# A softmax kernel's two places where stores follow loads: a small head on the store replaced by a small tail on the load

## The chip, the cores and the metric

The kernel runs on one core of one Trainium2 chip. The metric is device time in microseconds (us). Before the change it is 163.16 us, the median of 3 runs (162.55 to 163.5).

## What is computed

The input `x` has shape 16 x 1024 x 512 in float32, that is 16,384 rows of 512. Each row is divided by a temperature of 0.5 and goes through a softmax:

```python
x_scaled = x / temp                                   # temp = 0.5
x_max = np.max(x_scaled, axis=-1, keepdims=True)
exp_x = np.exp(x_scaled - x_max)
return (exp_x / np.sum(exp_x, axis=-1, keepdims=True)).astype(np.float32)
```

33.55 MB are read from HBM and 33.55 MB are written to it.

## The kernel before

The rows are cut into 8 chunks (0 to 7) of 128 partitions x 16 rows x 512. A partition's 16 rows lie one after another in HBM, so a whole chunk is 4096 KB, and each partition's part of it is one run of 32 KiB. Six SBUF tiles hold chunks (`BUFS = 6`). Chunks 6 and 7 are loaded into the tiles of chunks 0 and 1, and must wait until those are stored.

The order of the work is written out by hand, engine by engine. For each block (chunk 0 is worked on in three blocks, chunk 7 in two, the others whole):

- `shift` (L74 to L82), VectorE (DVE): the negated maximum of every row (L78), then times 2 (L82).
- `exponentials` (L103 to L118), ScalarE (ACT): for each row, exp(2x - 2max) in place, with the sum of the row (L109).
- `scale_vector` (L121 to L132), DVE: the reciprocal of the sums (L126), then 14 of 16 rows are multiplied by it (L128). `scale_scalar` (L134 to L143), ACT: the other rows (L139).
- `store` (L145 to L154): the chunk goes to HBM once its last block is done (L152).

All loads (L71) and all stores (L152) are issued by SyncE (SP), in one queue, in this order: the loads of chunks 0 to 5 at the start; store 0; store 1; the load of chunk 6 (waits until store 0 has landed); the load of chunk 7 (waits until store 1 has landed); stores 2 to 7. SP issues in order, so an instruction of its that waits holds up all that stand behind it. A DMA takes its turn in the queue once it is issued. There are thus two places in the queue where a store comes directly after a load: load 5 then store 0, and load 7 then store 2. And one where a load comes after a store: store 1 then load 6.

`LOADS` says how each chunk's load is cut: chunk 0 in three (rows 0 to 3, 4 to 7, 8 to 15), chunks 1 to 6 whole, chunk 7 without its last row. That row is loaded by GpSimd (POOL) in `load_last_row` (L89 to L101), through another queue (q0), when ACT is at row 10 of chunk 5.

`STORES` says how each store is cut, in columns of a partition's 16 x 512 values. Stores 0 and 2 use `LEAD`: a first DMA of 128 columns (512 bytes of each partition, 64 KB in all, "the head"), then a second with the rest (32,256 bytes of each partition, 4032 KB). The others are one DMA each (32,768 bytes of each partition). A partition's part of a DMA is one packet in the trace, and 8 partitions go through each of the 16 DMA engines. Each DMA ends with a completion packet of 4 bytes on each engine; it has landed when all 16 have been written.

SP's DMAs count their completions in eight semaphores, taken in turn; the ninth DMA uses the first one's again, and waits until the first has landed.

Of the kernel before, what the change touches and what calls it, by code (L numbers as in the profile page):

```python
# [1 line left out]

# [4 lines left out]


@with_exitstack
def kernel(  # L10
    ctx: ExitStack,
    tc: tile.TileContext,
    x: bass.AP,
    out: bass.AP,
):
    nc = tc.nc
    fp32 = mybir.dt.float32
    P = nc.NUM_PARTITIONS
    AX = mybir.AxisListType.X
    EXP = mybir.ActivationFunctionType.Exp  # L20
    COPY = mybir.ActivationFunctionType.Copy
    MAX = mybir.AluOpType.max

    D = x.shape[-1]
    xf = x.flatten_outer_dims()
    of = out.flatten_outer_dims()
    N = xf.shape[0]

    G = 16
    C = N // (P * G)
    assert C * P * G == N
    xr = xf.rearrange("(c p g) d -> c p g d", p=P, g=G)
    outr = of.rearrange("(c p g) d -> c p g d", p=P, g=G)
    WHOLE = [(0, G)]
    LOADS = [[(0, 4), (4, 8), (8, G)]] + [WHOLE] * 6 + [[(0, G - 1)]]
    BLOCKS = [[(0, 4), (4, 8), (8, G)]] + [WHOLE] * 6 + [[(0, 8), (8, G)]]

    LEAD = [(0, D // 4), (D // 4, G * D)]
    ALL = [(0, G * D)]
    STORES = [LEAD, ALL, LEAD] + [ALL] * 5
    BMAX = 16
    BUFS = 6

    data = ctx.enter_context(tc.tile_pool(name="data", bufs=BUFS))
    stats = ctx.enter_context(tc.tile_pool(name="stats", bufs=6))

    ctx.enter_context(tc.manual_schedule())  # L50


    warm = stats.tile([P, 1], fp32, name="warm", bufs=1)
    zero = nc.const_aps.tensor(0.0, (P, 1), fp32)
    nc.scalar.activation(out=warm, in_=zero, func=EXP)  # L55

    chunks = {}
    blocks = [(c, lo, hi) for c in range(C) for lo, hi in BLOCKS[c]]
    n = len(blocks)
    biases, sums, recips = {}, {}, {}  # L60

    finished = []

    def load(c):
        if c < BUFS:
            chunks[c] = data.tile([P, G, D], fp32, name="xt")
        else:
            chunks[c] = chunks[c - BUFS]
        xt = chunks[c]
        for lo, hi in LOADS[c]:  # L70
            part = nc.sync.dma_start(out=xt[:, lo:hi, :], in_=xr[c][:, lo:hi, :])  # L71
            finished.append(part.ins.name)

    def shift(i):  # L74
        c, lo, hi = blocks[i]
        b = hi - lo
        negmax = stats.tile([P, BMAX], fp32, name="negmax")
        nc.vector.tensor_reduce(  # L78
            negmax[:, 0:b], chunks[c][:, lo:hi, :], axis=AX, op=MAX, negate=True
        )  # L80
        biases[i] = stats.tile([P, BMAX], fp32, name="bias")
        nc.vector.tensor_scalar_mul(biases[i][:, 0:b], negmax[:, 0:b], 2.0)  # L82

    def load_last_row(signal):  # L89
        seen = stats.tile([P, 1], fp32, name="seen", bufs=1)  # L90
        copied = nc.gpsimd.tensor_copy(out=seen, in_=signal)  # L91
        finished.append(copied.ins.name)
        c = C - 1
        halves = "p (h d) -> p h d"
        to = chunks[c - BUFS][:, G - 1, :].rearrange(halves, h=2)
        of_ = xr[c][:, G - 1, :].rearrange(halves, h=2)
        for p0, p1 in ((P - 2, P), (0, P - 2)):
            part = nc.gpsimd.dma_start(  # L98
                out=to[p0:p1], in_=of_[p0:p1], max_dma_last_dim=2 * D
            )  # L100
            finished.append(part.ins.name)  # L101

    def exponentials(i, rows):  # L103
        c, lo, hi = blocks[i]
        if i not in sums:
            sums[i] = stats.tile([P, BMAX], fp32, name="sums")
        for g in rows:
            row = chunks[c][:, lo + g, :]
            nc.scalar.activation(  # L109
                out=row,  # L110
                in_=row,
                func=EXP,
                bias=biases[i][:, g : g + 1],
                scale=2.0,
                accum_out=sums[i][:, g : g + 1],
            )
            if c == BUFS - 1 and g == 10:
                load_last_row(sums[i][:, g : g + 1])  # L118


    def scale_vector(i):  # L121
        c, lo, hi = blocks[i]
        b = hi - lo
        k = b - b // 8
        recips[i] = stats.tile([P, BMAX], fp32, name="recip")
        nc.vector.reciprocal(recips[i][:, 0:b], sums[i][:, 0:b])  # L126
        rows = chunks[c][:, lo : lo + k, :]
        last = nc.vector.tensor_mul(  # L128
            rows, rows, recips[i][:, 0:k].unsqueeze(2).broadcast_to((P, k, D))
        )  # L130
        if i == n - 1:
            finished.append(last.ins.name)  # L132

    def scale_scalar(i):  # L134
        c, lo, hi = blocks[i]
        b = hi - lo
        for g in range(b - b // 8, b):
            row = chunks[c][:, lo + g, :]
            last = nc.scalar.activation(  # L139
                out=row, in_=row, func=COPY, scale=recips[i][:, g : g + 1]  # L140
            )
            if i == n - 1:
                finished.append(last.ins.name)  # L143

    def store(i):  # L145
        c, _, end = blocks[i]
        if end < G:
            return
        to = outr[c].rearrange("p g d -> p (g d)")
        of_ = chunks[c].rearrange("p g d -> p (g d)")  # L150
        for lo, hi in STORES[c]:
            part = nc.sync.dma_start(out=to[:, lo:hi], in_=of_[:, lo:hi])  # L152
            if c < C - 1:
                finished.append(part.ins.name)  # L154

    for c in range(BUFS):
        load(c)

    def rows(i):
        c, lo, hi = blocks[i]
        return range(hi - lo)

    shift(0)
    shift(1)
    exponentials(0, rows(0))
    for i in range(n):
        if i + 1 < n:
            exponentials(i + 1, rows(i + 1))  # L170
        scale_vector(i)
        scale_scalar(i)
        if i + 2 < n:
            shift(i + 2)
        store(i)
        c, _, hi = blocks[i]
        if hi == G and c == 1:
            load(BUFS)
            load(BUFS + 1)

    seen = nc.sync.nop()
    info = mybir.DependencyInfo(
        mybir.DependencyClass.Sync, mybir.DependencyReason.DATA
    )
    for name in finished:
        tc.add_manual_dep(seen.ins, name, info, reason="leaves one wait for the end")


# [1 line left out]
_INS = ['x']  # L190
_OUTS = [((16, 1024, 512), 'float32')]


# [23 lines left out]
```

## Time and profile before

| what | us |
|---|---|
| median of 3 runs | 163.16 (162.55 to 163.5) |
| the profiled execution's own time | 162.63 |
| its span, first to last instruction | 160.9 |
| DVE busy | 134.7 (84%) |
| ACT busy | 101.9 (63%) |
| DMA queue q1 (SP's): share of 16 engines' span | 97.4% |
| moved over the span | 67.13 MB, 417 GB/s |

The DMA queue is fullest: its packets fill 97.4% of the time of the 16 DMA engines. The SP timeline shows when each DMA was issued; the list of DMA issues shows how long after that the last of its 16 completions came, and their sum is the landing time. Where the queue always holds work, the interval from one landing to the next is the time that the slowest engine spent on that DMA. The packet records of the trace give the start, duration and size of each packet; they do not say which engine carried it.

### The profile page before, as it was taken

What the parts mean: (1) busy time and instruction counts of PE and PEld (TensorE: products, weight loads), DVE (VectorE), ACT (ScalarE), POOL (GpSimd) and SP (SyncE); (2) the same over time, 40 slices, a digit from 0 to 9 for tenths busy, and PEclk for the clock granted to TensorE, in tenths of its full rate; (3) what the DMA queues carried; (4) which work ended last, traced back from release to release, by engine and by line L of the source; (5) the groups of instructions that cost most, each with busy time, mean ns of one, the idle gap of its engine ahead of it and who ended that gap; (6) DMA issues with size and microseconds to landing.
All of it is one profiled execution on the core that took longest, in us unless ns stands there. A gap on an engine that the chain in (4) does not pass through costs nothing.

```text
span 160.9 us, 418 instructions
## 1 busy us (share of the span) xinstructions
DVE 134.7 (84%) x44; ACT 101.9 (63%) x273; POOL 1.9 (1%) x7
## 2 busy tenths in 40 slices
DVE  0589949999999999999999999999999999772000
ACT  3095490099899927993699459963999942950000
POOL 0000000000000000000000000300000000000000
DMA  5999999999999999999999999999999999999993
GB/s 183 444 428 493 407 407 489 407 391 491 407 407 464 432 399 393 393 428 473 399 424 473 394 466 411 410 466 439 416 416 432 456 416 432 456 416 416 464 416 139
DMA packets 3010, 67.13 MB, mean 417 GB/s; under 512 B 376, under 2 KB 632, under 8 KB 704
## 3 DMA queue, kind: packets, MB, share of 16 engines
q1 hardware_dynamic: 2880, 66.85, 97.4%
q0 software_dynamic: 128, 0.26, 0.4%
q14 instruction: 2, 0.02, 0.0%
HBM read 33.55 MB, written 33.55 MB: 417 GB/s over the span
## 4 chain that ended last, share of the span: by engine, by line
DVE 68%; DMA 13%; issue 5%; ACT 3%; SPq 1%
DVE negmax L78 38%; DVE xt L128 29%; DMA xt<-in_x_dram 13%; ACT xt L109 3%; DVE recip L126 1%; DVE bias L82 1%; SPq L71 1%
## 5 line engine op out<-in xcount | busy, mean ns | idle before, releaser
L109 ACT ACTIVATE xt<-xt,bias 128x512 f32<-128x512 f32 x128 | 90.4, 708 | 40.1 <-DVE bias L82 40.1
L78 DVE TENSOR_REDUCE negmax<-xt 128x16 f32<-128x8192 f32 (+2 forms) x11 | 69.9, 6352 | 7.9 <-DMA xt<-in_x_dram 7.9
L128 DVE TENSOR_TENSOR xt<-xt,recip 128x7168 f32<-128x7168 f32 (+2 forms) x11 | 62.0, 5636 | 0.4
L109 ACT ACTIVATION_READ_ACCUMULATOR xt<-xt,bias 128x1 f32 x128 | 24.0, 187 | 0.0
L139 ACT ACTIVATE xt<-xt,recip 128x512 f32<-128x512 f32 x15 | 9.9, 707 | 0.0
L126 DVE RECIPROCAL recip<-sums 128x16 f32<-128x16 f32 (+2 forms) x11 | 2.4, 219 | 2.3 <-ACT xt L109 2.3
L82 DVE TENSOR_SCALAR bias<-negmax 128x16 f32<-128x16 f32 (+2 forms) x11 | 1.9, 173 | 0.4
L55 ACT ACT_TABLE_LOAD x1 | 1.3, 1283 | 0.7 <-PEq L201 0.7
L98 POOL DMA_DIRECT2D xt<-in_x_dram x2 | 1.5, 741 | 0.6 <-issue 0.6
L91 POOL COPY seen<-sums 128x1 f32<-128x1 f32 x1 | 0.2, 184 | 102.0 <-ACT xt L109 102.0
L55 ACT ACTIVATE warm<-const-float32-0.0 128x1 f32<-128x1 f32 x1 | 0.2, 203 | 0.0
L201 POOL MEMSET const-bfloat16-1.0<- 128x1 bf16 x1 | 0.1, 96 | 0.0
L201 POOL MEMSET const-uint8-127<- 128x1 uint8 x1 | 0.1, 96 | 0.0
L201 POOL MEMSET const-float32-0.0<- 128x1 f32 x1 | 0.1, 93 | 0.2 <-issue 0.2
L201 POOL MEMSET const-float32-1.0<- 128x1 f32 x1 | 0.1, 93 | 0.0
## 6 DMA issues: line engine op xcount, KB each, us to landing
xt<-in_x_dram SPq DMA_DIRECT2D x6, 4096.0 KB, 34.4
out_dram<-xt SPq DMA_DIRECT2D x6, 4096.0 KB, 21.5
out_dram<-xt SPq DMA_DIRECT2D x2, 4032.0 KB, 28.6
xt<-in_x_dram SPq DMA_DIRECT2D x1, 3840.0 KB, 19.5
xt<-in_x_dram SPq DMA_DIRECT2D x2, 1024.0 KB, 6.1
xt<-in_x_dram SPq DMA_DIRECT2D x1, 2048.0 KB, 11.5
xt<-in_x_dram POOLq DMA_DIRECT2D x1, 252.0 KB, 13.7
out_dram<-xt SPq DMA_DIRECT2D x2, 64.0 KB, 34.2
```

The lines of the kernel that those rows point to most:

```text
L55: nc.scalar.activation(out=warm, in_=zero, func=EXP)
L71: part = nc.sync.dma_start(out=xt[:, lo:hi, :], in_=xr[c][:, lo:hi, :])
L78: nc.vector.tensor_reduce(negmax[:, 0:b], chunks[c][:, lo:hi, :], axis=AX, op=MAX, negate=True)
L82: nc.vector.tensor_scalar_mul(biases[i][:, 0:b], negmax[:, 0:b], 2.0)
L91: copied = nc.gpsimd.tensor_copy(out=seen, in_=signal)
L98: part = nc.gpsimd.dma_start(out=to[p0:p1], in_=of_[p0:p1], max_dma_last_dim=2 * D)
L109: nc.scalar.activation(out=row, in_=row, func=EXP, bias=biases[i][:, g : g + 1], scale=2.0, accum_out=sums[i][:, g : g + 1],)
L126: nc.vector.reciprocal(recips[i][:, 0:b], sums[i][:, 0:b])
L128: last = nc.vector.tensor_mul(rows, rows, recips[i][:, 0:k].unsqueeze(2).broadcast_to((P, k, D)))
L139: last = nc.scalar.activation(out=row, in_=row, func=COPY, scale=recips[i][:, g : g + 1])
L201: nc = _bacc.Bacc("TRN2", target_bir_lowering=False, num_devices=1)
```

## The change

Load 5 is cut in two DMAs: rows 0 to 14 (30,720 bytes of each partition), then row 15 (2,048 bytes of each partition, 256 KB in all, "the tail"). Load 7, which had rows 0 to 14 in one DMA, is cut into rows 0 to 13 (28,672 bytes) and row 14 (2,048 bytes). Stores 0 and 2 become one DMA each of 32,768 bytes of each partition. The number of DMAs on SP's queue stays 20. The rest of the program is the same but for which semaphores are waited for.

```diff
     WHOLE = [(0, G)]
-    LOADS = [[(0, 4), (4, 8), (8, G)]] + [WHOLE] * 6 + [[(0, G - 1)]]
+
+    LOADS = [[(0, 4), (4, 8), (8, G)]] + [WHOLE] * 4
+    LOADS += [[(0, G - 1), (G - 1, G)], WHOLE, [(0, G - 2), (G - 2, G - 1)]]
     BLOCKS = [[(0, 4), (4, 8), (8, G)]] + [WHOLE] * 6 + [[(0, 8), (8, G)]]
-
-    LEAD = [(0, D // 4), (D // 4, G * D)]
     ALL = [(0, G * D)]
-    STORES = [LEAD, ALL, LEAD] + [ALL] * 5
+    STORES = [ALL] * 8
```

SP's queue around the two places, with bytes of each partition:

| place | before | after |
|---|---|---|
| load 5, store 0 | 32,768; 512; 32,256 | 30,720; 2,048; 32,768 |
| load 7, store 2 | 30,720; 512; 32,256 | 28,672; 2,048; 32,768 |

## The prediction

> **What bounds the kernel now.** First the page's busy slices and its DMA queues.
>
> ```profile
> DVE  0589949999999999999999999999999999772000
> ACT  3095490099899927993699459963999942950000
> DMA  5999999999999999999999999999999999999993
> q1 hardware_dynamic: 2880, 66.85, 97.4%
> ```
>
> DMA is at 9 in every slice but the first and the last; DVE begins after it and stops 15 us before the end. SP's queue q1 alone fills 97.4% of the 16 engines' span. The chain of work that ended last is put down to DVE for 68%, so the question is whether compute ever leaves the queue empty. The last store is the one that could be late: in the timeline SP issues it at 145.78, and the store ahead of it in the queue lands at 150.4 (issued 131.28, 19.1 us to landing). So every store stands in the queue before its turn, the last with 4.6 us to spare, and the time is that of one stream through the DMA engines.
>
> Next, the list of DMA issues, one stretch per issue. Issue time (SP timeline) plus the last column is the landing.
>
> ```profile
> xt<-in_x_dram SPq DMA_DIRECT2D x1, 4096.0 KB, 48.3
> ...
> xt<-in_x_dram SPq DMA_DIRECT2D x1, 4096.0 KB, 58.5
> ...
> out_dram<-xt SPq DMA_DIRECT2D x1, 64.0 KB, 49.1
> ...
> out_dram<-xt SPq DMA_DIRECT2D x1, 4032.0 KB, 28.7
> ...
> out_dram<-xt SPq DMA_DIRECT2D x1, 4096.0 KB, 25.0
> ...
> xt<-in_x_dram SPq DMA_DIRECT2D x1, 4096.0 KB, 20.0
> ...
> xt<-in_x_dram SPq DMA_DIRECT2D x1, 3840.0 KB, 19.5
> ...
> out_dram<-xt SPq DMA_DIRECT2D x1, 64.0 KB, 19.3
> ...
> out_dram<-xt SPq DMA_DIRECT2D x1, 4032.0 KB, 28.4
> ```
>
> These are load 4, load 5, head 0, rest of store 0, store 1, load 6, load 7, head 2, rest of store 2, issued at 3.83, 4.34, 13.88, 43.82, 57.27, 72.61, 82.25, 82.68, 83.16. The trace's record of completions gives the landings in hundredths: 52.13, 62.83, 63.02, 72.55, 82.23, 92.60, 101.73, 101.99, 111.59. The steps between them are what the slowest engine spent: load 5 10.70, head 0 0.19, rest 9.53, store 1 9.68, load 6 10.37, load 7 9.13, head 2 0.26, rest 9.60. Undisturbed 4096 KB steps are 9.71 (loads 1 to 2) and 9.65 to 9.70 (stores 5 to 7).
>
> So **load 5, at the first of the two places, costs 0.98 more than 8 packets of 1213 ns (9.70) and a completion explain; load 7, at the second, costs nothing more** (8 x 1138 ns = 9.10, measured 9.13). The packet records place the first loss: on every engine the last one or two 32,768-byte packets of load 5, between 58.0 and 62.5, take 1.35 to 2.08 us in place of 1.21, and the head's 512-byte packets after them take their usual 27 ns. Summed over 16 engines it is 13.8 us, 0.86 per engine. Around 98 to 102, two packets are long, by 0.28 in all. Load 6's extra 0.65 is one engine alone, the slowest: its first packet +0.44, its last +0.27.
>
> **The change, part by part.** All durations are packet records of this execution: 32,768 B 1213 ns, 32,256 B 1194, 30,720 B 1138, 16,384 B 611, 512 B 27, a completion 9; and 2,048 B, in POOL's row load, 84. A 28,672-byte packet isn't in the trace; between 16,384 and 30,720 the slope is 527 ns for 14,336 B, so I estimate 1063.
>
> Removed, per engine: a head is 8 x 27 + 9 = 225 ns, and the rest 8 x 1194 = 9552, against 8 x 1213 = 9704 for a whole store. One head costs 225 + 9552 - 9704 = 73 ns, two 146. The landings agree: 0.19 + 9.53 = 9.72, against 9.65 to 9.70.
>
> Added, per engine: load 5's tail costs 8 x (1138 + 84) + 9 - 9704 = 81 ns; load 7's, 8 x (1063 + 84) + 9 - 9104 = 81 ns. Two are 162. On the slowest engine the head's packets come with gaps of 20 ns; if the tail's do, it is 8 x 20 = 160 ns more each, and 160 less each for the heads. **Net of the packets: +0.016 us**, with ends of -0.3 and +0.35.
>
> The Trainium skill ("DMA: Bandwidth & Descriptors", Anatomy of one DMA) fits a DMA as 2.0 us plus bytes at 436 GB/s, and its rules for authors say to coalesce small transfers into large ones, which speaks against any tail of 256 KB. The rows of head 0 and head 2, DMAs of 64 KB, show 0.19 and 0.26 in a full queue, so the fixed part lies beside other transfers here; by the page's fit two tails would be 4.0 us more and two heads 4.0 us less, also nothing net.
>
> SP's queue. An issue takes 0.33 to 0.49 us of SP, which waits for most of the span. Load 5's tail is the ninth DMA, so it waits for the first load (landed 5.78); behind it on SP stand store 0 (issued 43.82) and store 1. Its turn in the ring is after 61. Cover 55 us. If that cover were gone, the ring would idle. Load 7's tail waits for the semaphore of load 3 (landed 42.41); SP gets to it after 82.6, so the wait is over. Store 2 moves back behind it by one issue, about 0.4 us, to 83.1 in place of 82.7; its turn is near 101.7. Store 4 now waits for load 5's tail too, landed by 63, and is issued at 107. Store 0 goes out when the rest of it did, 43.82, 18 us before its turn; the early issue of the head at 13.88 bought nothing. Load 6 waits for store 0 (72.55) and is issued 9.6 us before its turn. POOL's and its row load's place don't change.
>
> Compute. ACT's row 15 of chunk 5 and row 14 of chunk 7, and DVE's maxima of those blocks, wait for one semaphore more. The tails land with the loads they belong to, near 63 and 102; DVE reaches chunk 5's maxima at 85.64 at the earliest and chunk 7's last block at 131.14. No price while the queue leads by 20 us.
>
> So all that is disputed is what happens at the two places. For a switch from loads to stores with a small head the trace has two rows: 0.98 and 0.0. For a small tail and a whole 32,768-byte store it has none. Ends: the tail makes both free (-0.98), or each costs what the first does now, so the second gains it (+0.98), or the first doubles as well (+1.96). I take **0 change at both**. The loss at the first place lies on load packets that are ahead of the head, and the same head gives no loss at the second place; so the head doesn't decide it. What differs is that it is the first store of the program; it stays so. That is argued, not shown.
>
> **The sum** on the profiled execution's own time: 162.63 + 0.02 = 162.65. The median of the runs is 0.53 above that execution, so the forecast against the median is 163.16 + 0.02, rounded to **163.2**. Own range, with the packet ends: 162.85 to 163.5.
>
> **Rivals.**
>
> Slower, the second place loses its cover: the small head is why the switch at 101 is free, because only a small packet has to find its way to HBM before the next can follow, and a tail on the load side doesn't do that. For it: the second place has a head and no loss. Against: the first has one and loses 0.98. Price: one stall as at the first place, 163.16 + 0.98 = 164.1; if the first place also doubles, 165.1. It decides from a loss of 0.82 (0.5%) at either place.
>
> Faster, the stall is a share of the last big load packets: the last one or two packets of each engine were long, by up to 0.86 for 32,768 bytes. If what precedes the first store is 2,048-byte packets, the loss shrinks with them: 163.16 - 0.9 = 162.3. For it: the loss stops exactly at the packets of 512 bytes. Against: the loss reaches two packets back, and 30,720-byte packets would stand there still. If the slowest engine's lag, 0.64 behind the second slowest at the end (160.02 and 159.38 in the completions of the last store), also went, 161.7.
>
> The change does nothing because the tail isn't separate work for the engines: the packets are then 8 and 8 as counted, and it is the forecast's case with 163.2.
>
> **How the numbers follow.** A measurement of this kernel can tell about 0.5% from no change, that is 0.82 us: bounds 162.34 and 163.98. The forecast's case, with the third rival in it, has 0.50, all of it within. The slower rival has 0.30, of which 0.28 is over the bound; the faster one 0.20, of which 0.18 is over it. So faster 0.18, same 0.54, slower 0.28. The range reaches from the faster rival's 162.2 to beyond one stall at 164.3; the doubled stall and the lost lag are left out.
>
> **What would show it.** In the profile after: q1's packets 2880 as before and 66.85 MB; the step of load 5 with its tail about 10.8 and that of load 7 with its tail about 9.2; stores 0 and 2 at 9.7 each. Long packets at 58 to 62 again and none at 98 to 102. Wrong if the step of load 7 plus tail is near 10, or if load 5 plus tail is near 9.8, or if store 0 or 2 itself takes over 10: then the small packets decide the switch. A last store issued after the store ahead of it has landed would refute that compute has slack.

## The result, and the profile after

The changed kernel takes 164.39 us (median of 7 runs, 163.68 to 164.45), the kernel before 163.16 (7 runs, 162.36 to 163.5). The ratio is 1.0063 with a 95% interval of 1.0041 to 1.0085: slower by 1.03 us, between 0.67 and 1.39. The forecast was 163.2, no change.

The page of the changed kernel, to be set beside the slices and the queue line shown for before:

```profile
DVE  0689949999999999999999999999999999580000
DMA  5999899899999989998998999999999999999990
GB/s 182 444 448 476 387 452 452 387 462 436 396 468 412 446 294 438 452 452 387 460 444 387 464 445 405 424 410 432 442 468 395 444 452 404 452 436 420 452 412 16
q1 hardware_dynamic: 2880, 66.85, 96.7%
```

The same packets and bytes as before, spread over more time (97.4% then). The last slice is the thing to see. It starts at 158.3, and only 16 GB/s move in it; in the page of before the last slice holds 139, with a 3 in the DMA row where this one has 0:

```profile
GB/s 183 444 428 493 407 407 489 407 391 491 407 407 464 432 399 393 393 428 473 399 424 473 394 466 411 410 466 439 416 416 432 456 416 432 456 416 416 464 416 139
```

For some 3 us at the end of the changed kernel nearly all DMA engines are done and something is still awaited.

The list of DMA issues of the changed kernel, one stretch per issue, from load 6 to store 2. SP issued them at 72.94, 82.66, 83.04 and 83.58:

```profile
xt<-in_x_dram SPq DMA_DIRECT2D x1, 4096.0 KB, 20.1
...
xt<-in_x_dram SPq DMA_DIRECT2D x1, 3584.0 KB, 20.0
...
xt<-in_x_dram SPq DMA_DIRECT2D x1, 256.0 KB, 20.3
...
out_dram<-xt SPq DMA_DIRECT2D x1, 4096.0 KB, 29.6
```

Issue plus landing gives 93.0, 102.7, 103.3 and 113.2. From load 6 to the end of store 2 that is 20.15 us in the completions, where the packets alone explain 18.90 (8 x 1063 + 9, 8 x 84 + 9, 8 x 1213 + 9 ns). Before, the same place took 18.99, with 18.90 explained as well.

The page can't say whose time that is. The record of the 16 completions of each DMA, one from each engine, can: the last one against the median of the 16. Below, "the slowest engine" is the one that completes last, "the median engine" the median of the 16, and the "lag" the time between them.

| landing (us) | before: median, last | after: median, last |
|---|---|---|
| load 4 | 51.51, 52.13 | 51.52, 52.17 |
| store 0 | 71.70, 72.55 | 71.87, 72.92 |
| load 6 | 91.14, 92.60 | 91.26, 93.01 |
| store 2 | 110.17, 111.59 | 110.36, 113.16 |
| store 7 | 159.05, 160.02 | 159.33, 161.56 |

**The median engine ends 0.28 later, the last one 1.54 later.** One engine is behind the others, and the change puts it further behind: by 0.2 at the first place and by 1.1 at the second. In the packet records the step at the second place is a single packet: a 28,672-byte packet of load 7 that starts at 98.94 and takes 2374 ns in place of 1063.

One warning on these two profiles. The profiled execution of before took 162.63, below most of its runs, that of the changed kernel 164.45, the highest of its runs, near their median. Their difference, 1.82, is more than the change costs.

Why one engine is behind is partly in the trace: the queue q14 has two packets of 8 KB inside the span, instruction fetches. In a stretch of the trace of before, 34 to 39:

```profile
q1 hardware_dynamic: 71, 2.33, 108.2%
q14 instruction: 1, 0.01, 0.4%
```

The fetch is at 36.42 and lasts 309 ns. The only long packet of that time, 32,768 bytes at 36.73, takes 382 ns more than its 1213. The other fetch is at 90.36, with a packet at 90.66 that is 269 ns too long. All fourteen profiles of this study have both pairs. That they are on the engine that ends last is inferred from its completions, since packet records name no engine.

**Not all of the cost is in the span.** A run takes longer than its span from first to last instruction: by 1.72 to 1.83 us in the 114 runs of before that stand beside the experiments below, and by 2.03 to 2.11 in the 7 of the changed kernel. So about 0.27 of the 1.03 us lies outside the span, where none of the program's DMAs runs: the first is issued and the last lands inside it. About 0.76 us (0.40 to 1.12) is left for the queue.

### The profile page after: what moved, and what is told of

It is laid out like the page before. It is cut to its first block, busy times and chain, and to the rows that moved or that the text cites. A ratio compares the mean times of both kernels' runs of the same rounds, so it can differ in the third digit from the quotient of the medians.

```text
span 162.4 us, 416 instructions
## 1 busy us (share of the span) xinstructions
DVE 134.7 (83%) x44; ACT 101.9 (63%) x273; POOL 1.9 (1%) x7
## 4 chain that ended last, share of the span: by engine, by line
DVE 63%; DMA 13%; issue 10%; ACT 3%; SPq 1%
DVE negmax L78 37%; DVE xt L128 24%; DMA xt<-in_x_dram 13%; ACT xt L109 3%; DVE recip L126 1%; DVE bias L82 1%; SPq L71 1%
```

## The experiments

Each kernel was timed in 5 rounds against the kernel before on the same chip. Ratios are to that.

What a run takes beyond its span is the same in all runs of a kernel within about 0.1 us, but not in all kernels. The medians are 1.76 to 1.79 us for before, plain, second place only, four tails, before with three rows and early head; 2.04 to 2.06 for after, both, first place only, halves and after with three rows; and 2.19 for tails elsewhere and relief ahead. So 0.27 of what the second group costs, and 0.41 of what the third does, is outside the span. It goes in part with VectorE's instructions in the trace, waits included: 53 in the first group, 54 in the second, 55 in the third, but four tails, in the first group, has 57. The cause is open. "Inside the span" below is the time by the ratio less this part.

**The four corners.** Theory A: the small head makes the switch from loads to a store cheap, and the change lost it. Theory B: the small tail on the load costs, and the head does nothing.

Neither head nor tail ("plain"):

```diff
-    STORES = [LEAD, ALL, LEAD] + [ALL] * 5
+    STORES = [ALL] * 8
```

> Neither head nor tail: whole loads, whole stores, 18 DMAs on the queue. Theory A, the missing head is the cost (the tail is neutral): as the changed kernel, about 1.0 slower than before, near 164.2, and the step of load 7 (9.13 before) is near 10.2 on the slowest engine. Theory B, the tail is the cost (the head is neutral): as before, 163.2 within 0.3, and load 7 steps 9.1.

Measured 163.46, ratio 1.0011 (0.9989 to 1.0034). Theory A falls in its size: the two lost heads cost 0.2 us at the centre, 0.55 at most. But load 7 stepped 9.66 on the slowest engine, not the 9.1 of theory B, so that step is not the tail's alone.

Head and tail together ("both"):

```diff
-    LOADS = [[(0, 4), (4, 8), (8, G)]] + [WHOLE] * 6 + [[(0, G - 1)]]
+    LOADS = [[(0, 4), (4, 8), (8, G)]] + [WHOLE] * 4
+    LOADS += [[(0, G - 1), (G - 1, G)], WHOLE, [(0, G - 2), (G - 2, G - 1)]]
```

> Tail on loads 5 and 7 and head on stores 0 and 2. Theory A (missing head costs): as before plus 0.16 of packets, 163.3, with load 7 and its tail together near 9.2. Theory B (tail costs): about 1.0 slower, near 164.2, with load 7 and its tail together near 10.3.

Measured 163.89, ratio 1.0050 (1.0029 to 1.0071): with both heads kept, the tails cost nearly what the whole change costs, 0.82 us of time and 0.55 (0.20 to 0.89) inside the span. For theory B, and against A's 163.3. Load 7 with its tail took 9.96 on the slowest engine.

The change at the first place alone (tail on load 5, whole store 0), then at the second alone (tail on load 7, whole store 2):

```diff
+    LOADS = [[(0, 4), (4, 8), (8, G)]] + [WHOLE] * 4 + [[(0, G - 1), (G - 1, G)]] + [WHOLE] + [[(0, G - 1)]]
+    STORES = [ALL, ALL, LEAD] + [ALL] * 5
```

> Only the first place changed: tail on load 5, whole store 0; load 7 and store 2 as before. From the two profiles, load 5 to store 0 took 20.42 before and 20.75 after, so 0.3 of the loss should be here: 163.5. If the loss is at whichever place lacks a head, both theories give this. If it were spread evenly over the places: 163.7.

```diff
+    LOADS = [[(0, 4), (4, 8), (8, G)]] + [WHOLE] * 6 + [[(0, G - 2), (G - 2, G - 1)]]
+    STORES = [LEAD, ALL, ALL] + [ALL] * 5
```

> Only the second place changed: tail on load 7, whole store 2; load 5 and store 0 as before. From the two profiles, load 7 to store 2 took 19.00 before and 20.16 after, so 1.2 of the loss should be here: 164.2, and one engine should have a packet of load 7 that is about 1.3 us too long. If that long packet was an accident of the one profiled execution: 163.3.

Measured 163.88, ratio 1.0036 (1.0009 to 1.0062), and 163.47, ratio 1.0020 (0.9998 to 1.0043). The two sum to 0.56%, near the change's 0.63%. Inside the span they cost the same, 0.32 and 0.33 us, each within some 0.4, where the two profiles gave 0.3 and 1.2. The long packet of 1.3 us was there in the second kernel (2429 ns for 28,672 bytes), and yet its median hardly rose. And the first kernel, whose second place is that of before, had one too (1900 ns for 30,720 bytes, at 99.42). So the long packet isn't made at the second place by the edit there.

**Is the long packet an accident of an execution?** The kernel before again, unchanged:

> The kernel before once more, unchanged, for a second profile and for the width of the comparison: ratio 1.000 within 0.002. If the slowest engine's long packet at the second place (0.6 to 1.4 us in all five profiles with a change, absent in the first profile of before) belongs to the tails and missing heads, it is absent here too. If it comes and goes with the execution, it is here in an execution near 163.5 and the profiles alone say little about it.

Measured 163.27, ratio 0.9996 (0.9975 to 1.0016); the profiled execution took 162.50 and shows no packet of load 7 more than 0.16 us too long. It was once more a short execution, so this alone leaves both readings open.

**Small packets, or any cut?** Loads 5 and 7 cut in the middle; then four tails each; then tails on loads 3 and 6, which another load follows, with the heads kept:

```diff
+    HALVES = [[(0, 8), (8, G)]]
+    LOADS = [[(0, 4), (4, 8), (8, G)]] + [WHOLE] * 4 + HALVES + [WHOLE] + [[(0, 8), (8, G - 1)]]
+    STORES = [ALL] * 8
```

> Whole stores; loads 5 and 7 are two DMAs, as in the changed kernel, but cut in the middle: 16 KiB of each partition, then 16 KiB (14 KiB for load 7). By packets it costs 0.08 us each. If an additional DMA in the load is what costs: as the changed kernel, 164.2. If it is the small packets just ahead of the store: as whole loads, 163.4 to 163.6.

```diff
+    def four(end):
+        return [(0, end - 4)] + [(g, g + 1) for g in range(end - 4, end)]
+    LOADS = [[(0, 4), (4, 8), (8, G)]] + [WHOLE] * 4 + [four(G)] + [WHOLE] + [four(G - 1)]
+    STORES = [ALL] * 8
```

> Whole stores; loads 5 and 7 end with four rows of 2 KiB, each in a DMA of its own, in place of one. By packets alone 0.32 us for each load, 0.63 in all: 163.46 + 0.63 = 164.1. If each small tail adds the stall that the one tail seems to add (0.3 to 0.4 us): 165.5 to 166.

```diff
+    TAIL = [[(0, G - 1), (G - 1, G)]]
+    LOADS = [[(0, 4), (4, 8), (8, G)]] + [WHOLE] * 2 + TAIL + [WHOLE] * 2 + TAIL + [[(0, G - 1)]]
```

> The heads stay on stores 0 and 2; the tails are on loads 3 and 6, each followed by another load. By packets 0.16 us: 163.4. If a tail costs wherever it is: as with both, 163.9 to 164. If it costs only where a store follows: 163.4.

Measured: halves 164.01, ratio 1.0039 (1.0017 to 1.0062); four tails 163.47, ratio 1.0015 (0.9992 to 1.0037); tails elsewhere 163.60, ratio 1.0012 (0.9995 to 1.0029). Theory B falls as it was put. Inside the span a cut in the middle, with no small packet, costs 0.37 us (0.01 to 0.74), and four tails on each load 0.23 (-0.13 to 0.60), where their packets, less those of the two lost heads, make 0.48. A stall with each small tail, 165.5 to 166, is refuted. Tails elsewhere cost nothing that can be seen there: the 0.20 us of time is less than the 0.41 that lies outside the span.

The runs of the four tails suggest what kind of thing is at work: six lie between 162.84 and 163.29, six between 163.64 and 164.47. The halves have one run at 162.38 and the other eleven from 163.81 to 164.47. The profile of the halves is that one: the engine that fetches is 0.74 behind at load 6, and nothing is long at the second place.

**The lag theory.** So I formed another: the slowest engine loses 0.4 to 1.4 us at the second place in executions in which it comes there too far behind. All fourteen profiles, those of the experiments below among them, ordered by that lag (last completion of load 6 less the median one). The loss is the slowest engine's time from there to the end of store 2, less the sum of its packets:

| kernel | profiled run (us) | lag at load 6 (us) | loss at the second place (us) |
|---|---|---|---|
| relief ahead (below) | 163.62 | 0.54 | 0.03 |
| halves | 162.38 | 0.74 | 0.13 |
| before, again | 162.50 | 1.25 | 0.17 |
| before | 162.63 | 1.47 | 0.09 |
| second place only | 163.81 | 1.48 | 1.28 |
| before, three rows by POOL | 163.20 | 1.55 | 1.30 |
| both | 163.92 | 1.61 | 0.85 |
| early head | 163.74 | 1.65 | 1.03 |
| after | 164.45 | 1.75 | 1.25 |
| first place only | 163.93 | 1.78 | 0.70 |
| four tails | 164.47 | 1.84 | 0.95 |
| tails elsewhere | 163.99 | 1.95 | 0.44 |
| after, three rows by POOL | 164.17 | 2.02 | 1.36 |
| plain | 163.79 | 2.16 | 0.64 |

No row with a lag up to 1.47 loses more than 0.17, and none above it less than 0.44, with heads or tails or neither. The kernels "second place only" and "before, three rows" are the kernel before up to load 6, and lie on the other side of that line than its own two profiles. Where the line is, and that there is one, isn't shown: 1.47 without a loss and 1.48 with one are two kernels that differ in load 7 itself, and above the line the loss doesn't grow with the lag. What the table does show is that the loss isn't tied to an edit at the second place: first place only, early head and tails elsewhere have load 7 and store 2 as before and lose there, halves and relief ahead have them cut otherwise and don't.

**Relief behind the place.** POOL's queue carries nearly nothing on the slowest engine (its step of store 3 is 9.75 in the trace of before, the median's 10.20), so more rows by that queue relieve it. The last three rows of chunk 7 in place of one, in the kernel before and in the changed one:

```diff
-    LOADS = [[(0, 4), (4, 8), (8, G)]] + [WHOLE] * 6 + [[(0, G - 1)]]
+    LOADS = [[(0, 4), (4, 8), (8, G)]] + [WHOLE] * 6 + [[(0, G - 3)]]
...
-        to = chunks[c - BUFS][:, G - 1, :].rearrange(halves, h=2)
-        of_ = xr[c][:, G - 1, :].rearrange(halves, h=2)
+        to = chunks[c - BUFS][:, G - 3 :, :].rearrange(halves, h=2)
+        of_ = xr[c][:, G - 3 :, :].rearrange(halves, h=2)
```

> The kernel before, but POOL's queue loads the last three rows of chunk 7 in place of one, so load 7 has 13 rows. In every profile the slowest engine has almost no packets of that queue (its step of store 3 is 9.75 where the median engine's is 10.2). Theory of the one engine (the end is set by the engine that also fetches instructions; its lag of 0.8 to 2.2 at the end is most of the difference between runs): it is relieved of two rows, 16 packets' worth or 1.2 us, the others get 0.15 more; time falls by about 1.0, to 162.2, and the completions of the last store end within 0.5 of each other. If all engines set the end alike: no change, 163.3.

> The changed kernel with the same three rows by POOL's queue. Theory of the one engine: most of what the change costs is on that engine (1.26 of its 1.54 in the profiles, the median engine's end moved by 0.28), so with it relieved the changed kernel comes to within 0.2 to 0.5 of the other kernel of this call that has three rows: 162.5. If the change costs all engines alike: it stays 1.0 above that kernel.

Measured 163.12, ratio 0.9987 (0.9966 to 1.0007), and 163.83, ratio 1.0038 (1.0021 to 1.0055). What the theory of the one engine forecast, 162.2 and 162.5, is missed both times. The change still costs 0.51% between these two, 0.83 us, of which 0.28 is outside the span. The slowest engine did gain 1.6 us on the median one between stores 2 and 7 (its lag fell from 2.86 to 1.26), but in that profile it had lost 1.3 at the second place, which comes first, and it stayed the last. This relief comes too late to stop the loss.

**Relief ahead of the place.** The changed kernel, with the last row of chunk 6 by POOL's queue too (`last_row` is the part of `load_last_row` that loads the row of a chunk):

```diff
-    LOADS += [[(0, G - 1), (G - 1, G)], WHOLE, [(0, G - 2), (G - 2, G - 1)]]
+    LOADS += [[(0, G - 1), (G - 1, G)], [(0, G - 1)], [(0, G - 2), (G - 2, G - 1)]]
...
             load(BUFS)
+            last_row(BUFS)
             load(BUFS + 1)
```

> The changed kernel, with the last row of chunk 6 also loaded through POOL's queue, issued when store 0 has landed (about 73), so that the slowest engine is relieved of 0.6 us ahead of the second place and not only behind it. Theory of the carried lag: the slowest engine loses 0.4 to 1.2 us more at the second place in executions in which it comes there over 1.5 behind the median engine; the change adds 0.2 to 0.3 to that lag. Relieved early it comes there 1.2 behind, loses nothing there, and the time falls from 164.4 to 162.6 to 163.0, below the kernel before. Rival, the tails cost by themselves, on every engine or wherever they stand: the time stays at 163.8 to 164.4, whatever the lag.

Measured 163.60, ratio 1.0005 (0.9991 to 1.0020). Landings of load 6, load 7 and its tail, from issues at 72.70, 82.54 and 82.92:

```profile
xt<-in_x_dram SPq DMA_DIRECT2D x1, 3840.0 KB, 20.0
...
xt<-in_x_dram SPq DMA_DIRECT2D x1, 3584.0 KB, 18.7
...
xt<-in_x_dram SPq DMA_DIRECT2D x1, 256.0 KB, 18.9
```

And the page's slices and rates:

```profile
DMA  5999999999999899999999999999999999999993
GB/s 187 447 438 471 406 422 471 406 424 463 414 414 464 381 365 422 414 398 487 426 378 422 430 405 455 442 399 432 419 487 414 398 503 398 398 503 398 406 495 130
```

Load 7 with its tail steps 9.15 (10.31 in the changed kernel), and the last slice is full again as in before, 130 against 16. The lag is 0.54 and nothing is lost, with the tails in place: in this profile the mechanism is as the lag theory says. The time is not: 163.6, where 162.6 to 163.0 was expected. Of what is missing, 0.41 is outside the span; inside it the kernel is 0.32 us faster than before (0.07 to 0.55). The median engine ends at 160.04, 0.71 later than in the changed kernel: 0.38 between load 4 and store 0, ahead of the relief; 0.43 between store 1 and load 6; less 0.1 elsewhere. In load 6 the packets that start from 82.4 to 84.6 are 120 to 180 ns longer, while POOL's row comes in. The rival's 163.8 to 164.4 is missed too, by less. The same relief in the kernel before wasn't tried, so the 0.58% that it takes off can't all be booked to the tails.

No kernel here beats the kernel before in time beyond the interval.

**The first place.** Its loss of 0.8 on every engine was put down in the prediction to the program's first store. A head early in the queue:

```diff
-    STORES = [LEAD, ALL, LEAD] + [ALL] * 5
+    STORES = [LEAD[1:], ALL, LEAD] + [ALL] * 5
...
-    for c in range(BUFS):
+    for c in range(4):
         load(c)
...
+        if i == 0:
+            lo, hi = LEAD[0]
+            part = nc.sync.dma_start(
+                out=outr[0].rearrange("p g d -> p (g d)")[:, lo:hi],
+                in_=chunks[0].rearrange("p g d -> p (g d)")[:, lo:hi],
+            )
+            finished.append(part.ins.name)
+            load(4)
+            load(5)
```

> The kernel before with loads 4 and 5 issued after the head of store 0, so that the first store of the program stands in the queue after load 3, near 42 us, and the rest of store 0 comes directly after load 5. If the 0.8 us that every engine loses at the first place belongs to the program's first store, it is lost at load 3 (step 10.5 in place of 9.7) and load 5 steps 9.7. If it belongs to the change from loads to a long run of stores: load 5 steps 10.5 again, load 3 9.7. Time 163.3 either way, 164.1 if both cost.

Measured 163.58, ratio 1.0005 (0.9982 to 1.0028). The list of DMA issues, for the head (issued at 13.70) and load 4 (14.09):

```profile
out_dram<-xt SPq DMA_DIRECT2D x1, 64.0 KB, 28.9
...
xt<-in_x_dram SPq DMA_DIRECT2D x1, 4096.0 KB, 38.2
```

The head lands at 42.60, 0.18 after load 3, and load 4 at 52.27, 9.67 later: the first store of the program, as a head of 64 KB, costs nothing beyond its packets. Load 5, just ahead of the long stores, steps 10.83 as ever. So the loss stays ahead of the first long stores, and isn't that of a first store of any size. Whether it is the change from loads to long stores, the first such change, or something at that time of the run isn't shown; at the second place the same change costs the median engine hardly anything.

## Where the prediction was right and where it was wrong, point by point

- **That one stream through the DMA engines sets the time, and compute has slack**: right. The last store is issued at 145.61, 6.3 us before the one ahead of it lands.
- **SP's queue and the added waits cost nothing**: right. The tail of load 7 went out at 83.04 and store 2 at 83.58, where 83.1 was forecast.
- **Net of the packets +0.016**: not contradicted, and not measured. The median engine's end, which shows it best, moved by 0.28, heads taken away alone (plain) give 0.2 at the centre, and tails put elsewhere -0.2 inside the span, with intervals that hold zero. The ends of this sum rest on gaps of 20 ns between the head's packets on the slowest engine; the trace of before has none, as these packets start 23 to 24 ns apart and last 27. The small DMAs' fixed part stayed hidden: the tails landed 0.64 and 0.66 after the rows ahead of them, where the packets explain 0.68. The fit of the Trainium skill ("DMA: Bandwidth & Descriptors", Anatomy of one DMA) with 2.0 us for each DMA, which the page gives for DMAs issued by GpSimd, isn't seen for SyncE's in this full queue.
- **"I take 0 change at both" places: this step failed.** It measured 0.16 on the median engine and 0.33 on the last at the first place, and 0.07 and 1.16 at the second. So the sign that the prediction gave against itself came, a step of load 7 plus tail near 10 (10.31), but not for its reason: the halves, with no small packet, cost too. The step took what one execution of 162.63 showed for what the places cost. The second place's "0.0" in that execution is probably not what most runs of before have, which no profile of a longer one shows: 24 of 114 runs of before in the four sets of experiments are under 163.0, and both of its profiled executions, 162.63 and 162.50, are so short. The prediction saw the slowest engine fall behind (0.65 at load 6, 0.64 behind the second slowest at the end) and used that in the faster rival only.
- **What the sum has no term for**: what a run takes beyond its span, 0.27 of the 1.03 us. The prediction added its packets to a time that it took as otherwise fixed.
- **"It is the first store of the program"**: refuted by the early head, for a first store of 64 KB.
- **The slower rival**, 164.1, was near the number and at the right place, with the wrong mechanism: it made the head the cover, but without heads and tails the time is within 0.34% of before, and with heads kept the tails still cost 0.5%, a third of it outside the span. Heads do something small at the first place: beyond its packets the median engine loses 0.64 to 0.77 there in the six profiles with a head between load 5 and store 0, and 0.60 to 1.22 in the other eight, seven of them over 0.77.
- **The range**, 162.2 to 164.3: by the ratio (163.16 x 1.0063 = 164.19) the time is inside, the median of the changed kernel's own runs 0.09 above. That is luck: the upper end was there for a stall of every engine at the second place, and what came instead is one engine's loss and a part outside the span.

What stays open: what sets the 0.27 us outside the span; why a large lag costs the slowest engine another 0.4 to 1.4 us; and that the change makes executions with such a lag more common, which is argued from the spread of the runs (none of its 7 is under 163.6), since only before has two profiles and every other kernel one.

## What to carry to other kernels

When a queue of transfers sets the time, the end is that of its slowest engine: compare the last completion of each DMA with the median one before pricing an edit by sums. Set the time of every run beside its span, too: a part that differs between two programs outside the span is no effect of their queues. A profile of one execution may lack a loss that most runs have; look where its own time stands among the runs, and take a second profile before calling a place free. An edit that came to 16 ns in packets cost 1 us here: a quarter of it outside the span, and the rest, by the two profiles, mostly on an engine that was already behind.

## What the runs showed of the hardware

An instruction fetch of 8 KB went with a packet that was 0.26 to 0.38 us too long, twice in each of the fourteen profiles, by its completions on the engine that ends last. POOL's transfer of a row left that engine nearly free (store 3 stepped 9.75 on it, 10.20 on the median engine), and more rows by that queue took 1.6 us off its lag. At about 60 us, where loads give way to long stores, the median engine lost 0.6 to 1.2 us; at about 100 us, where they do so again, 0.3 at most. A 64 KB store between two loads cost only its 0.18. The time outside the span was near 1.78, 2.05 or 2.19 us, for each program the same within about 0.1.
